# First-set raw weights in four own tiles, decode products at the pair's end, and several steps moved

## The chip, the cores and the metric

One core of a Trainium2 chip runs the kernel. The metric is the device time of one execution in microseconds (us); lower is better. Engines are named as in the profile: PE does matrix products, DVE and ACT element-wise work, POOL general work, SP issues most DMA transfers.

## The reference

One step of a decoder layer in float32. A prompt of 2048 tokens (width 1024) and 8 single new tokens ("samples", which carry states) go through one mixer: norm, one input projection to 8 groups of 512 columns, two recurrences, one output projection, a residual and a final norm.

```python
h = rmsnorm(x, norm_g)
rq, rk, rv, rg, hq, hf, hi, hgate = jnp.split(h @ w_in, 8, axis=-1)
rq = rotary(rq, pos);  rk = rotary(rk, pos) * RET_DK ** -0.5
o_ret, s_ret_new = chunked_decay_recurrence(rq, rk, rv, log_gamma, s_ret)   # one decay per head
o_ret = head_rmsnorm(o_ret, ret_g) * silu(rg)
logf = logaddexp(log(lb), log1p(-lb) + log_sigmoid(hf));  kin = (1 - lb) * sigmoid(-hf)
o_hg, s_hg_new = chunked_decay_recurrence(silu(hq), kin, hi, logf, s_hg)    # one decay per channel
o_hg = head_rmsnorm(o_hg, hg_g) * silu(hgate)
y = rmsnorm(x + concat([o_ret, o_hg]) @ w_out, final_norm_g)                # and the four new states
```

Each recurrence is S_t = diag(f_t) S_(t-1) + k_t v_t^T, o_t = S_t^T q_t, over 4 heads of 128 channels. For the samples it is one such step from the given states ("decode").

## The kernel before, in words

**Products.** float32 operands are split in two parts, high and low; a product is three matmuls (`three`, L350): high x high, high x low, low x high. Projections are done for a pair of token blocks at a time by a Strassen-Winograd scheme of seven products (`v_pair`, list `CHAIN`: A11 B11, A12 B21, S2 T2, S1 T1, S3 T3, S4 B22, A22 T4), each 12 matmuls of 128x512. B is weights, T sums of weights, A tokens, S sums of tokens.

**Stages.** 24 pairs run in three sets of eight: the first set (pairs 0 to 7) projects the value columns, the second and third the retention columns; beside the third set run the retention steps (`r_steps`, its p is the pair less 16). Then eight units (half, head) of the HGRN recurrence, whose projections, in groups of six matmuls, are the fill; then the output projection, again in pairs with seven products each.

**Order.** PE runs in the order of the code. In a set, `after[n]` lists what is called once product n of a pair has been written (half numbers: in the middle of the next). DVE, ACT and SP are put in order by a scheduler when the kernel is built; `behind(f)` has what f issues follow the last instructions of DVE, ACT and SP that are written so far. In the HGRN stage each unit's work is a list of (fraction, step), and `merge` writes a step into the fill once the fraction of the fill is done. `MOVE` shifts single steps there: key (half, head, level).

**Buffers.** A tile takes the next buffer of its pool and tag, and whoever writes it first waits for the last reader of the tile that had it. Pool `rawp` has six buffers of 512 KB for raw weights, raw tokens (xr) and sums (S). Pool `ps_o`, tag "o", has two buffers in the matrix engine's memory; the state updates (pu), the chunk outputs (po) and the decode products (pd4 to pd7, pgd) of the HGRN stage and of the first set take them in turn.

**First set.** Token blocks come in as xn; their squares (ACT, `stats_sum`) give the norms; PE spreads the row sums (prs). In pairs 2 to 5, `wg_load` loads two rows-of-blocks of the second set's raw weights (wgr, product B and its sums), `wg_decode` multiplies the samples by them (pgd, 16 small matmuls by `four`), and `wg_spool` makes their sums (`w_sums`, four DVE operations) and stores these (ws1T).

**HGRN.** The recurrence of a unit works in levels: bursts of 64 small products (plh) give scores of sub-blocks; after each, DVE updates kh and qqh in place and copies scores by a mask into Abh, and ACT copies kh and qqh (kepth) for the next. The burst of level 1 and of level 3 (`levels2`) of some units takes a decode product with it (`then_decode`, `d_mm`): dS times the sample's query, into pd; pd6 goes with unit (1,1), level 3. The outputs of the unit before run at the same time: puh (state), poh (output of a chunk; h100 is half 1, head 0, chunk 0), ACT squares of it, DVE obh (output times norm), PE poth (transposed).

**Retention and output.** `r_flip` transposes rk (pkt), `r_score` makes scores (par, DVE rA), `r_out` the outputs (por). `d_tr` transposes the decode outputs `do` (pdt); `wd_at` places it in an output pair.

## Time and profile before

| | us |
|---|---|
| median of three runs | 1028.8 (1026.54 to 1030.4) |
| the profiled execution | 1030.97 |
| its span (first to last instruction) | 1029.1 |
| PE busy | 1014.0 |
| DVE busy | 734.2 |
| ACT busy | 550.3 |
| POOL busy | 122.8 |

The profile comes from one execution; times in it are us from the span's start. Rows of the timeline are start, length, engine, line, operation, output<-inputs, shape and count; a bracket tells how long the engine stood idle before it and what it waited for. Waits are listed as engine, tile and line, released by engine, tile and line: total, number, longest. Buffer numbers are left out, so plh113 reads plh. The mean granted clock of PE is 0.998 of full.

### The profile page before, as it was taken

How to read it: one execution, taken by the hardware profiler on the slowest of the kernel's cores; microseconds unless marked ns; L12 is line 12 of the kernel's file. 1: busy time of each engine (PE TensorE's matmuls, PEld its weight loads, DVE VectorE, ACT ScalarE, POOL GpSimd, SP SyncE). 2: the span in 40 equal slices, each digit the busy share in tenths (PEclk: the TensorE clock that was granted, in tenths of full speed). 3: DMA queues.
4: the chain of work that ended last, by engine and by line, in shares of the span. 5: the costliest groups of instructions: out<-in, count | busy, mean ns of one | idle time of the engine just before them, and what ended most of it. 6: DMA issues, size and time to landing. Idle time of an engine off the chain costs nothing.

```text
span 1029.1 us, 21541 instructions
## 1 busy us (share of the span) xinstructions
PE 1014.0 (99%) x8366; PEld 841.7 (82%) x8366; DVE 734.2 (71%) x1353; ACT 550.3 (53%) x1211; POOL 122.8 (12%) x231
## 2 busy tenths in 40 slices
PE   9999999999999999999999999999999999999997
PEld 7767778887778888888888899898888878878775
DVE  7887666888675885576666768768768576667886
ACT  7863435735434765555564665667556476433242
POOL 0200001000000101111111100111022112301122
PEclk9999999999999999999999999999999999999999
DMA  8699998878999965567766697555864496565652
GB/s 290 210 327 330 332 334 275 326 263 313 312 326 304 359 238 184 189 226 247 233 222 205 210 334 268 193 185 200 283 216 133 129 362 227 180 252 204 227 186 103
DMA packets 151271, 255.63 MB, mean 248 GB/s; under 512 B 11424, under 2 KB 79280, under 8 KB 151040
## 3 DMA queue, kind: packets, MB, share of 16 engines
q1 hardware_dynamic: 141408, 225.03, 64.7%
q0 software_dynamic: 7440, 24.76, 6.3%
q10 hardware_dynamic: 2320, 4.46, 1.2%
q8 instruction: 66, 1.08, 0.4%
q14 instruction: 37, 0.30, 0.1%
HBM read 166.51 MB, written 87.69 MB: 247 GB/s over the span
## 4 chain that ended last, share of the span: by engine, by line
PE 82%; DMA 4%; DVE 1%; issue 0%; SPq 0%; POOLq 0%; ACT 0%; POOL 0%; DVEq 0%; ACTq 0%
PE po L350 10%; PE pjqh L1032 9%; PE pjfh L1032 8%; PE py L1659 4%; PE plh L1246 2%; PE pur L741 1%; PE par L734 1%; PE puh L1115 1%; PE por L747 1%; PE por L749 1%; PE poh L1131 1%; DMA oT1h<-t_dramh 1%; PE poh L1133 1%; PE pv20a L350 1%; PE pv21a L350 1%; PE pv22a L350 1%
## 5 line engine op out<-in xcount | busy, mean ns | idle before, releaser
L1032 PE MATMUL pjfh<-xh,w_h 128*128 128x512 f32 (+2 forms) x160 | 59.4, 372 | 0.0
L1032 PE MATMUL pjqh<-xh,w_h 128*128 128x512 f32 (+2 forms) x160 | 58.9, 368 | 0.0
L1226 ACT ACTIVATE kepth<-kh 128x1024 f32<-128x1024 f32 x24 | 25.4, 1060 | 62.0 <-DVE kh L1216 62.0
L1032 PE MATMUL pjqh<-xh,w_l 128*128 128x512 f32 (+2 forms) x160 | 55.7, 348 | 0.0
L1032 PE MATMUL pjfh<-xh,w_l 128*128 128x512 f32 (+2 forms) x160 | 55.7, 348 | 0.0
L1032 PE MATMUL pjfh<-xl,w_h 128*128 128x512 f32 (+2 forms) x160 | 55.6, 348 | 0.0
L1032 PE MATMUL pjqh<-xl,w_h 128*128 128x512 f32 (+2 forms) x160 | 55.6, 347 | 0.0
L1216 DVE TENSOR_TENSOR kh<-kh,fph 128x512 f32<-128x512 f32 x48 | 33.4, 696 | 22.8 <-PE plh L1246 19.8
L118 DVE TENSOR_TENSOR ab_l<-xr,ab_h 128x512 fp32r<-128x512 f32 (+1 forms) x40 | 37.5, 954 | 11.6 <-ACT ab_h L117 11.6
L772 DVE SCALAR_TENSOR_TENSOR obr<-por,omr,rg 128x128 f32<-128x128 f32 x64 | 18.0, 344 | 33.3 <-POOL omr L764 28.2
L762 ACT ACTIVATE obr<-por 128x128 f32<-128x128 f32 x64 | 16.8, 277 | 44.4 <-PE por L749 40.6
L117 ACT ACTIVATE ab_h<-xr 128x512 fp32r<-128x512 f32 (+1 forms) x40 | 32.4, 838 | 11.3 <-DVE xr L302 11.3
L1032 PEld LDWEIGHTS pjqh<-xh,w_h 128*128 128x128 f32 x160 | 30.4, 190 | 4.8 <-issue 1.2
L1032 PEld LDWEIGHTS pjfh<-xh,w_h 128*128 128x128 f32 x160 | 30.2, 189 | 4.1 <-issue 0.4
L1032 PEld LDWEIGHTS pjqh<-xh,w_l 128*128 128x128 f32 x160 | 30.1, 188 | 4.1
L1032 PEld LDWEIGHTS pjfh<-xh,w_l 128*128 128x128 f32 x160 | 30.1, 188 | 4.0
L409 ACT ACTIVATE vo<-vo 128x512 f32<-128x512 f32 x32 | 20.1, 629 | 24.7 <-DVE vo L403 10.8
L1219 DVE TENSOR_TENSOR qqh<-qqh,fph 128x512 f32<-128x512 f32 x48 | 32.8, 683 | 0.0
L1032 PEld LDWEIGHTS pjqh<-xl,w_h 128*128 128x128 f32 x160 | 30.2, 189 | 3.0
L1032 PEld LDWEIGHTS pjfh<-xl,w_h 128*128 128x128 f32 x160 | 30.2, 189 | 2.7
L302 DVE SCALAR_TENSOR_TENSOR xr<-xr,g_in,rb 128x256 f32<-128x256 f32 x64 | 27.1, 480 | 7.3 <-DMA xr<-in_x_t 4.2
L1659 PE MATMUL py<-woh,oc_h 128*128 128x512 f32 x64 | 26.6, 415 | 0.0
(1839 smaller groups left out, 3335.0 us busy)
## 6 DMA issues: line engine op xcount, KB each, us to landing
xr<-a_dram SPq DMA_DIRECT2D x24, 512.0 KB
S<-s_dram SPq DMA_DIRECT2D x24, 512.0 KB
xn<-in_x_prompt SPq DMA_DIRECT2D x32, 256.0 KB
xr<-in_x_t SPq DMA_DIRECT2D x16, 512.0 KB
a_dram<-xr SPq DMA_DIRECT2D x16, 512.0 KB
s_dram<-S SPq DMA_DIRECT2D x16, 512.0 KB
wgr<-in_w SPq DMA_DIRECT2D x16, 512.0 KB
xr<-a_dram SPq DMA_DIRECT2D x32, 256.0 KB
```

The lines of the kernel that those rows point to most:

```text
L117: act.activation(h, src, AF.Copy)
L118: dve.tensor_tensor(l, src, h.bitcast(F32), op=ALU.subtract)
L302: dve.scalar_tensor_tensor(r[:, k], r[:, k], g_in[:, kk : kk + 1], spread_to[i], op0=ALU.mult, op1=ALU.mult)
L350: pe.matmul(ps, xx, ww, start=(first and n == 0), stop=(last and n == 2), skip_group_check=more)
L409: act.activation(o, src, AF.Silu)
L772: dve.scalar_tensor_tensor(o[:, cc], po[:, h], ms[:, h : h + 1], rb_of[c, "g"][:, cc], op0=ALU.mult, op1=ALU.mult)
L1032: pe.matmul(ps, ww[:, kk], x[:, k, b0 : b0 + n], start=(k == 0 and i == 0), stop=(k == KT - 1 and i == 2),)
L1216: dve.tensor_tensor(kv[:, :, 0, :], kv[:, :, 0, :], two[:, :, 1:2].to_broadcast([P, nb, b]), op=ALU.mult)
L1219: dve.tensor_tensor(qv[:, :, 1, :], qv[:, :, 1, :], two[:, :, 0:1].to_broadcast([P, nb, b]), op=ALU.mult)
L1226: act.activation(ss[:, 512:], k[:, :HALF], AF.Copy)
L1246: pe.matmul(dst[32 * i : 32 * i + 32, c], kk, qq, start=True, stop=True)
L1659: pe.matmul(ps, o[:, kk], w[:, k % 4, i * 512 : (i + 1) * 512], start=(k == 0 and n == 0), stop=(k == KT - 1 and n == 2),)
```

## The change

It has six parts:

1. Six more small warm-up products (18 instead of 12).
2. In the first set, the raw weights of a pair (1 MB) lie in four tiles of their own (tags zh0, zl0, zh1, zl1, one buffer each) and come in four loads of 256 KB, instead of two loads of 512 KB into `rawp`. They are loaded after product 1, tied behind what is written so far, instead of after product 0. Decode products, sums and stores come after product 6, the pair's last, instead of after 4 (pair 3: 5).
3. The squares of the first half of a pair's tokens, and the load of the second half, move from after product 2 to after product 1 in pairs 3 to 5 (pair 2 had them there).
4. In the first retention step, `r_flip` and `r_score`/`r_update` move half a product later.
5. `MOVE` gets three entries: the bursts of unit (1,1) level 3, unit (1,2) level 1 and unit (0,3) level 1 come earlier in the fill.
6. `d_tr` moves from after product 4 of output pair 2 to after product 0 of output pair 3.

```diff
--- before.py
+++ after.py
@@ -82,7 +82,7 @@
     wu = ps_tr.tile([P, P], F32, tag="tr", name="wu")
     for n in range(14):
         pe.matmul(wu, ones, ones, start=True, stop=True)
-    for n in range(12):
+    for n in range(18):
         pe.matmul(wu[:32, :16], ones[:, :32], ones[:, :16], start=True, stop=True)
 
     zero = const.tile([P, 24], F32, name="zero")
@@ -500,11 +500,12 @@
             hi_lo(h, l, wr[k][:, ty])
 
     def w_sums(r0, r1):
-        dve.tensor_tensor(r0[:, 0], r0[:, 1], r0[:, 0], op=ALU.subtract)
-        dve.tensor_tensor(r0[:, 1], r1[:, 1], r0[:, 1], op=ALU.subtract)
-        dve.tensor_tensor(r1[:, 1], r1[:, 1], r0[:, 0], op=ALU.subtract)
-        dve.tensor_tensor(r1[:, 0], r1[:, 0], r1[:, 1], op=ALU.subtract)
-        return ("T2", r1[:, 1]), ("T3", r0[:, 1]), ("T1", r0[:, 0]), ("T4", r1[:, 0])
+        b11, b12, b21, b22 = (r[:, g] if hasattr(r, "shape") else r[g] for r in (r0, r1) for g in range(2))
+        dve.tensor_tensor(b11, b12, b11, op=ALU.subtract)
+        dve.tensor_tensor(b12, b22, b12, op=ALU.subtract)
+        dve.tensor_tensor(b22, b22, b11, op=ALU.subtract)
+        dve.tensor_tensor(b21, b21, b22, op=ALU.subtract)
+        return ("T2", b22), ("T3", b12), ("T1", b11), ("T4", b21)
 
     def wv_comb(k):
         for op, r in w_sums(wr[k], wr[k + 4]):
@@ -512,9 +513,14 @@
             hi_lo(h, l, r)
 
     def wg_load(n, k):
-        for kk in (k, k + 4):
-            wr[kk] = rawp.tile([P, 2, GW], F32, tag="raw", name=f"wgr{n}{kk}")
-            sp.dma_start(wr[kk].rearrange("p g n -> p (g n)"), a[f"w_{n}"][kk])
+        for j, kk in enumerate((k, k + 4)):
+            if n == 1:
+                wr[kk] = [vq.tile([P, GW], F32, tag=f"z{x}{j}", name=f"wgr{n}{kk}{x}") for x in "hl"]
+                for g, r in enumerate(wr[kk]):
+                    sp.dma_start(r, a[f"w_{n}"][kk, :, g * GW : (g + 1) * GW])
+            else:
+                wr[kk] = rawp.tile([P, 2, GW], F32, tag="raw", name=f"wgr{n}{kk}")
+                sp.dma_start(wr[kk].rearrange("p g n -> p (g n)"), a[f"w_{n}"][kk])
 
     pgd = {}
 
@@ -522,7 +528,8 @@
         if n not in pgd:
             pgd[n] = ps_o.tile([P, 256], F32, tag="o", name=f"pgd{n}")
         for kk in (k, k + 4):
-            four(pgd[n], xs[:, kk], wr[kk].rearrange("p a b -> p (a b)"), kk == 0, kk == KT - 1)
+            halves = wr[kk] if n == 1 else [wr[kk][:, g] for g in range(2)]
+            four(pgd[n], xs[:, kk], halves, kk == 0, kk == KT - 1)
 
     def wg_spool(n, k):
         for op, r in w_sums(wr[k], wr[k + 4]):
@@ -587,7 +594,10 @@
     def four(ps, x, w, first, last):
 
         for j in range(4):
-            pe.matmul(ps[32 * j : 32 * j + x.shape[1]], x, w[:, j * 256 : j * 256 + 256], start=first, stop=last)
+            ww = w[j // 2] if isinstance(w, list) else w[:, j // 2 * 512 : j // 2 * 512 + 512]
+            pe.matmul(
+                ps[32 * j : 32 * j + x.shape[1]], x, ww[:, j % 2 * 256 : j % 2 * 256 + 256], start=first, stop=last
+            )
 
     pvd = []
 
@@ -817,9 +827,9 @@
             put(0.5 if p > 1 else 1.5, lambda: r_turn(ca - 2))
         if p < N_V:
             put(3, lambda: r_load(ca, "q"), lambda: r_load(ca, "v"))
-            d = 0 if p else 0.5
+            d = 0 if p else 1
             put(3.5 + d, lambda: r_flip(ca))
-            put(4 + d if p else 6, lambda: r_load(ca, "g"))
+            put(4 if p else 6, lambda: r_load(ca, "g"))
             put(5 if 0 < p < N_V - 1 else 4.5 + d, lambda: r_score(ca), lambda: r_update(ca))
             if p:
                 put(6, lambda: r_out(ca), lambda: r_load(ca + 1, "q"), lambda: r_load(ca + 1, "v"))
@@ -937,7 +947,7 @@
                 at = 6
             after[at] += [lambda i=i: tok_load(i + 2)]
         if i + 2 < N_V:
-            after[1 if i == 2 else 2] += [lambda i=i: behind(lambda: stats_sum(i + 2, 0)), lambda i=i: stats_load(i + 2, 1)]
+            after[1] += [lambda i=i: behind(lambda: stats_sum(i + 2, 0)), lambda i=i: stats_load(i + 2, 1)]
             after[4] += [lambda i=i: behind(lambda: stats_sum(i + 2, 1)), lambda i=i: stats_end(i + 2)]
             if i + 3 < N_V:
                 after[5] += [lambda i=i: stats_load(i + 3, 0)]
@@ -948,8 +958,11 @@
             after[2] += [decode_spread]
         if m < 3:
             if 2 <= j < 6:
-                after[0] += [lambda m=m, k=j - 2: wg_load(m, k)]
-                after[5 if i == 3 else 4] += [lambda m=m, k=j - 2: wg_decode(m, k), lambda m=m, k=j - 2: wg_spool(m, k)]
+                if m == 1:
+                    after[1] += [lambda m=m, k=j - 2: behind(lambda: wg_load(m, k))]
+                else:
+                    after[0] += [lambda m=m, k=j - 2: wg_load(m, k)]
+                after[6 if m == 1 else 4] += [lambda m=m, k=j - 2: wg_decode(m, k), lambda m=m, k=j - 2: wg_spool(m, k)]
             if j == 7:
                 after[0] += [lambda m=m: behind(lambda: wg_decode_out(m))]
                 for n, (_, op, _) in enumerate(CHAIN):
@@ -1174,7 +1187,7 @@
         dve.tensor_copy(old, pools["S"][hd - NH])
         return old
 
-    MOVE = {(0, 0, 1): 0.065, (0, 1, 3): 0.065, (0, 2, 1): 0.065, (1, 0, 1): 0.125, (1, 3, 1): 0.11}
+    MOVE = {(0, 0, 1): 0.065, (0, 1, 3): 0.065, (0, 2, 1): 0.065, (1, 0, 1): 0.125, (1, 3, 1): 0.11, (1, 1, 3): -0.1, (1, 2, 1): -0.065, (0, 3, 1): -0.06}
 
     def hgrn_rec(half, h, u):
         name = f"h{half}{h}"
@@ -1874,7 +1887,8 @@
         wd_at[i] += [(st_, lambda n=n: wd_load(2 * n)), (st_, lambda n=n: wd_load(2 * n + 1))]
         i, st_ = ((4, 3), (5, 0), (5, 4), (6, 1))[n]
         wd_at[i] += [(st_, lambda n=n: wd_mm(2 * n)), (st_, lambda n=n: wd_mm(2 * n + 1))]
-    wd_at[2] += [(0, d_ms), (2, d_rs), (4, d_tr)]
+    wd_at[2] += [(0, d_ms), (2, d_rs)]
+    wd_at[3] += [(0, d_tr)]
     wd_at[p0] += [(1, lambda: t3_split(0)), (2, lambda: t3_split(1))]
     wd_at[5] += [(0, lambda: dec.update(y=y_load(a["x_sample"], NB, "d")))]
     wd_at[6] += [(2, wd_out)]
```

What moves on the engines is shown at two places. On PE, around the burst of unit (1,1), level 3 (`plh` is the burst, `pd` is pd6, `poh` the output of chunk 101, `pjqh` and `pjfh` the fill). Before:

```order
L1032 MATMUL pjqh_0_8713<-xl_7115,w_h 128x512
L1032 MATMUL pjqh_0_8713<-xh_7114,w_l 128x512
L1246 MATMUL plh_8732<-kepth_8627 32x16 x32
L1246 MATMUL plh_8732<-qqh_8027,kh_8026 32x16 x32
L590 MATMUL pd_8808<-dS_8497,dqp 32x256 x4
L1032 MATMUL pjqh_0_8713<-xh_7114,w_h 128x512
```

After:

```order
L1144 MATMUL poh_8706<-v_8088,Ah 128x128
L1146 MATMUL poh_8706<-sth_8533,qqh_7538 128x128
L1259 MATMUL plh_8727<-kepth_8649 32x16 x32
L1259 MATMUL plh_8727<-qqh_8049,kh_8048 32x16 x32
L598 MATMUL pd_8803<-dS_8519,dqp 32x256 x4
L1045 MATMUL pjqh_0_8819<-xh_7136,w_h 128x512
```

The burst and pd6 stood between two groups of fill; now they follow directly on poh101, and pd6 still follows directly on the burst.

On DVE at the same place (`obh` of poh_8657 or poh_8679 is chunk 100's, of poh_8684 chunk 101's; the masked copies read plh113). Before:

```order
L1146 SCALAR_TENSOR_TENSOR obh_8720<-poh_8657,orsh_8675,v_8064 128x128 x4
L845 TENSOR_TENSOR dv_8710<-dv_8710,dk 128x1024
L1216 TENSOR_TENSOR kh_8026<-kh_8026,fph_8429 128x32x16
L1219 TENSOR_TENSOR qqh_8027<-qqh_8027,fph_8429 128x32x16
L1252 COPY_PREDICATED Abh_8454<-lmask,plh_8732 128x16x8
L1252 COPY_PREDICATED Abh_8454<-lmask,plh_8732 128x8x16
L1216 TENSOR_TENSOR kh_8026<-kh_8026,fph_8429 128x16x32
L1219 TENSOR_TENSOR qqh_8027<-qqh_8027,fph_8429 128x16x32
L1146 SCALAR_TENSOR_TENSOR obh_8816<-poh_8684,orsh_8702,v_8068 128x128 x4
```

After:

```order
L1187 COPY oldh_8983<-S_5677 128x128
L1229 TENSOR_TENSOR kh_8048<-kh_8048,fph_8451 128x32x16
L1232 TENSOR_TENSOR qqh_8049<-qqh_8049,fph_8451 128x32x16
L1265 COPY_PREDICATED Abh_8476<-lmask,plh_8727 128x16x8
L1265 COPY_PREDICATED Abh_8476<-lmask,plh_8727 128x8x16
L1229 TENSOR_TENSOR kh_8048<-kh_8048,fph_8451 128x16x32
L1232 TENSOR_TENSOR qqh_8049<-qqh_8049,fph_8451 128x16x32
L1159 SCALAR_TENSOR_TENSOR obh_8826<-poh_8679,orsh_8697,v_8086 128x128 x4
L855 TENSOR_TENSOR dv_8816<-dv_8816,dk 128x1024
```

Chunk 100's four obh stood ahead of the two updates and the masked copies; now they stand behind the two updates, the copies and two more updates.

On SP, from the stores of one pair's sums to the next pair's raw weights, in pair 5 (`ws1T` stores of sums, `wgr` raw weights, `xr` and `xn` tokens, `v_dram` results). Before:

```order
L529 DMA ws1T_128<-wgr_1171 128x512
L529 DMA ws1T_129<-wgr_1169 128x512
L529 DMA ws1T_127<-wgr_1169 128x512
L529 DMA ws1T_130<-wgr_1171 128x512
L344 DMA v_dram_94<-vo_1309 128x512
L242 DMA xr_1312<-in_x_t 128x1024
L242 DMA xr_1313<-in_x_t 128x1024
L263 DMA xn_1316<-in_x_prompt 128x512
L263 DMA xn_1317<-in_x_prompt 128x512
L344 DMA v_dram_93<-vo_1332 128x512
L517 DMA wgr_1350<-in_w 128x1024
L517 DMA wgr_1352<-in_w 128x1024
```

After:

```order
L536 DMA ws1T_128<-wgr16l 128x512
L536 DMA ws1T_129<-wgr12l 128x512
L536 DMA ws1T_127<-wgr12h 128x512
L536 DMA ws1T_130<-wgr16h 128x512
L344 DMA v_dram_93<-vo_1381 128x512
L263 DMA xn_1392<-in_x_prompt 128x512
L263 DMA xn_1393<-in_x_prompt 128x512
L520 DMA wgr13h<-in_w 128x512
L520 DMA wgr13l<-in_w 128x512
L520 DMA wgr17h<-in_w 128x512
L520 DMA wgr17l<-in_w 128x512
L312 DMA a_dram_107<-xr_1314 128x1024
```

The two loads of 512 KB behind the xr and xn loads became four of 256 KB, behind the second two xn loads (which stood later); the xr loads and the first two xn loads stand ahead of the stores.

## The prediction

> **What bounds the kernel now.** I read the page's busy rows first, then the list of what PE (the matrix engine) waited for, then single stretches of the timeline. The busy rows say that PE is the bound nearly everywhere.
>
> ```profile
> span 1029.1 us, 21541 instructions
> PE 1014.0 (99%) x8366; PEld 841.7 (82%) x8366; DVE 734.2 (71%) x1353; ACT 550.3 (53%) x1211; POOL 122.8 (12%) x231
> ```
> ```profile
> PEclk9999999999999999999999999999999999999999
> ```
>
> PE works 1014 of 1029 us at full granted clock, and the change neither removes nor adds products that count. So the time can move only by waits of PE that go and waits that come. Those that the change touches are these (total us, times, longest us):
>
> ```profile
> PE pgd L590 <- DMA wgr<-in_w: 2.7, 5, 0.7
> PE pkt L726 <- DVE rk L375: 1.4, 1, 1.4
> PE pdt L1396 <- DVE do L1392: 1.2, 1, 1.2
> ...
> PE prs L288 <- POOL rs_all L114: 0.6, 1, 0.6
> ```
>
> Together 5.9 us: all that can be won here is little over 0.5% (5.1 us), about what a measurement of this kernel can tell from no change.
>
> **Decode products of the first set (pgd).** Before, they stand in the middle of pairs 2, 4 and 5 and late in pair 3, and wait for their weights. Of pair 2 and of pair 3, PE's timeline (start, length):
>
> ```profile
> 71.59 0.62 PE L590 MATMUL pgd<-wgr,pk 128*8 128x256 f32 x8 [0.40 <-DMA wgr<-in_w]
> 72.80 0.62 PE L590 MATMUL pgd<-wgr,pk 128*8 128x256 f32 x8 [0.60 <-DMA wgr<-in_w]
> 73.35 0.50 PE L350 MATMUL pv2c<-B22h,s21h 128*128 128x512 f32 x1
> ```
> ```profile
> 95.60 1.05 PE L590 MATMUL pgd<-wgr,pk 128*8 128x256 f32 x16
> 96.58 0.50 PE L350 MATMUL pv3a<-T4h,ab_h 128*128 128x512 f32 x1
> ```
>
> Pair 3 waits for nothing: from its burst to the next product are 0.98 us. Pair 2's burst takes 1.76, 0.78 more, after an idle 0.40: it loses 1.18 where its idle rows add up to 1.0. By that ratio the 2.7 us of the list are 3.2 us of PE time. All of it goes if the weights are there at the pair's end.
>
> Whether they are, SP decides, which issues in order. A tile is used by the products, then by four sums, then by a store, and only then loaded again. The old order had such a chain too, and the chain view of pair 5 shows it:
>
> ```profile
> 123.00 5.90 DMA ws1T<-wgr
> 128.90 0.02 issue
> 128.92 8.37 DMA wgr<-in_w
> ```
>
> The new order of SP puts two token loads (xn) ahead of the four weight loads of pairs 4 and 5. Their buffers are freed by ACT's squares, which in the new order follow ACT's eviction p of the pair's fourth product. In pair 5 of before these are the rows (ACT's p, SP's two xn, and the square that one of them released):
>
> ```profile
> 134.02 0.58 ACT L390 ACTIVATE p<-pv5c 128x512 f32<-128x512 f32 x1
> ```
> ```profile
> 140.43 1.08 SPq L263 DMA_DIRECT2D xn<-in_x_prompt  x2
> ```
> ```profile
> 144.88 0.63 ACT L269 ACTIVATE xn<-xn 128x512 f32<-128x512 f32 x1 [0.60 <-DMA xn<-in_x_prompt]
> ```
>
> On this clock: p ends at 134.6, two squares of some 0.8 end at 136.2, the xn loads are issued by then, and four weight loads at 0.54 (1.08 for two) bring the last to 138.5. The decode products come three products of 12 matmuls after the fourth; at 0.23 us a matmul (the fence around plh below) that is 134.0 + 8.3 = 142.3. So the last load has 3.8 us. The nearest row for 256 KB in this stretch is xn itself: issued at 140.43, it released ACT at 144.88, 4.4 us. That makes a wait of some 0.6 us in each of pairs 4 and 5. The far row is the 8.37 us of wgr, behind a fuller queue: 4.6 us each. I take the nearer one, since in the new order only the two xn stand in the queue ahead: 1.2 us of new wait, ends 0 and 9.2. Pairs 2 and 3 have no eviction ahead of their loads; nothing is counted.
>
> The Trainium skill, "DMA: Bandwidth & Descriptors", section "Anatomy of one DMA", fits 2.0 us plus bytes over 436 GB/s to one transfer of GpSimd's queue; an estimate by it for 256 KB is 2.6 us, which fits into 3.8 and would take 1.2 us off the sum. The xn row's 4.4 us, in the traffic of this stretch, decides against it here.
>
> **Squares earlier.** The first half's row sums come a product earlier for the tokens of pairs 5 to 7, so prs should not wait: -0.6, ends 0 and -0.6.
>
> **First retention step half a product later.** rk came 1.4 us after PE asked for pkt; six matmuls fill just that. Scores and updates (par) move as far, so they run at the same clock time as now, but por does not move and comes 1.4 us earlier:
>
> ```profile
> 370.48 0.86 DVE L736 SCALAR_TENSOR_TENSOR rA<-par,pk 128x128 f32<-128x128 f32 x3
> ```
> ```profile
> 374.09 1.05 PE L747 MATMUL por<-rv,rA 128*128 128x128 f32 x8
> ```
>
> por would come at 372.7, rA is done at 371.3, or 1.2 to 2.4 later if one or two splits of DVE slip in ahead (1.2 each, by the oT3l row below). I take -1.0, ends -1.4 and -0.7.
>
> **d_tr three products later.** pdt then stands well behind `do`: -1.2. Next in line are the splits oT3l, which end at 918.99 now:
>
> ```profile
> 916.63 2.36 DVE L118 TENSOR_TENSOR oT3l<-oT3l,oT3h 128x1024 fp32r<-128x1024 f32 x2 [0.71 <-ACT oT3h L117]
> ```
> ```profile
> 919.33 0.39 PE L350 MATMUL po<-oT3l,op2S2h 128*128 128x512 f32 x1
> ```
>
> Their product would ask at 918.1, when the first half (to 917.8) is done; -1.2 stands, the other end is -0.3.
>
> **Three level bursts joined to neighbours.** Groups of small fp32 products cost an entry and an exit, as around plh here, where the pace is 0.23:
>
> ```profile
> 789.50 0.39 PE L1032 MATMUL pjqh<-xl,w_h 128*128 128x512 f32 x1
> 789.73 0.39 PE L1032 MATMUL pjqh<-xh,w_l 128*128 128x512 f32 x1
> 790.05 0.70 PE L1246 MATMUL plh<-kepth 128*32 128x16 f32 x62
> ```
> ```profile
> 791.70 0.50 PE L1032 MATMUL pjqh<-xh,w_h 128*128 128x512 f32 x1
> 792.04 0.40 PE L1032 MATMUL pjqh<-xl,w_h 128*128 128x512 f32 x1
> ```
>
> 0.32 and 0.34 instead of 0.23 make 0.2 us a join; three are 0 to -0.6, and I take -0.4.
>
> **The new wait: pd6.** The burst of unit (1,1), level 3, takes the decode product pd6 with it, tied behind it. pd6 needs one of two buffers; its turn gives it poh100's, which is free when DVE has made the four obh of that chunk. Before, DVE had them done at 788.4, and pd6 ran at 791.1 with no wait:
>
> ```profile
> 787.29 1.12 DVE L1146 SCALAR_TENSOR_TENSOR obh<-poh,orsh,v 128x128 f32<-128x128 f32 x4 [2.44 <-POOL orsh L114]
> 788.33 1.22 DVE L845 TENSOR_TENSOR dv<-dv,dk 128x1024 f32<-128x1024 f32 x1
> 791.37 0.69 DVE L1216 TENSOR_TENSOR kh<-kh,fph 128x512 f32<-128x512 f32 x1 [1.82 <-PE plh L1246]
> 791.98 0.69 DVE L1219 TENSOR_TENSOR qqh<-qqh,fph 128x512 f32<-128x512 f32 x1
> 792.58 0.62 DVE L1252 COPY_PREDICATED Abh<-lmask,plh 128x128 f32<-128x128 uint8 x2
> 793.19 0.69 DVE L1216 TENSOR_TENSOR kh<-kh,fph 128x512 f32<-128x512 f32 x1
> 793.80 0.69 DVE L1219 TENSOR_TENSOR qqh<-qqh,fph 128x512 f32<-128x512 f32 x1
> 794.41 1.12 DVE L1146 SCALAR_TENSOR_TENSOR obh<-poh,orsh,v 128x128 f32<-128x128 f32 x4
> ```
> ```profile
> 791.15 0.62 PE L590 MATMUL pd<-dS,dqp 128*32 128x256 f32 x6
> ```
>
> In the new order of DVE chunk 100's obh stand behind six instructions of which the first waits for plh113, and PE goes straight from plh113 to pd6. The rows from 791.37 on are that very chain, with chunk 101's obh at its end: to 794.41 + 1.12 = 795.53 it takes 4.16 us. PE stands still for that, the projection fill queued behind pd6. ACT's part in it, a copy of kh between the two updates, follows four short squares of poh101, which are done in time. I take +4.2; the ends are 3.4 (the chain to 794.41 and one obh) and 5, if ACT comes late.
>
> **The rest.** Six more warm-up products:
>
> ```profile
> 6.05 0.93 PE L86 MATMUL wu<-ones 128*32 128x16 f32 x24
> ```
> ```profile
> 7.66 0.50 PE L350 MATMUL pv<-wv_l,ab_h 128*128 128x512 f32 x1 [0.23 <-DVE wv_l L118]
> ```
>
> The twelve of now (two rows each) take 0.9 us; six more take 0.45 ahead of the first real product, and PE waits for wv_l at the second, 7.66, in any case: 0, ends 0 and +0.4. dS7 and dv7 are loaded later, past a store on SP; pd7, a unit later, needs them long after; 0, ends 0 and +2, the latter if DVE stands at dv7 with chunk 101's obh behind it.
>
> **Sum.** -3.2 + 1.2 - 0.6 - 1.0 - 1.2 - 0.4 + 4.2 = -1.0 us. The profiled execution took 1030.97 us (its span and 1.9 us around it), 2.2 above the median of the runs; so 1030.0 against it, and 1027.8 as a median.
>
> **The rivals.**
>
> *No stall at pd6* (its buffer free in time): 5.2 less than nothing changed, 1023.6, and 1022.4 if the weights are in time too. For it: before, pd6 had 2.7 us to spare. Against: the new order shows six instructions ahead, which need plh113 itself.
>
> *Slower: the weights come late at the pair's end.* The place is SP in pairs 4 and 5: xn and its squares, then the loads. With 8.4 us from issue to landing PE waits 4.6 us in each, 9.2 instead of 1.2: 1035.8. From 4.9 us on (1.1 each) nothing is left of the gain, from 7.5 us on the kernel is slower by 0.5%. For it: 8.37 is a row of this very load. Against: SP's order had 3 MB of stores and loads between the first ws1T store and that load; the new one waits for those stores to land and has 0.5 MB of xn ahead.
>
> *The change does nothing at pgd*: the stretch is bound by DMA and 3.2 us of waits merely move. Then 1029.8. For it is the row
>
> ```profile
> 129.00:154.00 25.00, 24.36 (x120) 18.98 (x119) 15.28 (x26) 9.63 (x18) 1.08 (x3) 1.00 0.94 336
> ```
>
> with its DMA share of 0.94; against it, that the loads are now due 5 us later in the pair.
>
> *PE restarts slowly.* A gap of 4.2 us is three times the longest wait listed. If matmuls ran at half pace for as long after it, 2 to 4 us come on top: 1030 to 1032. The clock row shows no such case, since no gap was as long. The Trainium skill, "TensorE: Matmul & The Clock Gate", Part 1, says that PE's clock halves after one idle window of about 3.4 us; by that rule a gap of 4.2 may or may not cover a whole window. No run here shows it yet.
>
> **Chances.** The forecast 0.60, with a range of its own of 1025.5 to 1030; no stall 0.13; weights late 0.12; nothing at pgd 0.08; slow restart 0.07. Of no stall, most lies under 1023.7, so faster 0.11; of late weights, most lies over 1033.9, so slower 0.10; the rest, 0.79, within 0.5%. The range 1023 to 1033.5 leaves out the far parts of two rivals.
>
> **What would show it.** In the profile after: a wait of pd for obh of about 4.2 us, the longest of PE; pkt, pdt and prs gone from the list; pgd under 1.5 us; por with at most 0.6 of new wait. I am wrong if pd is not in the list, if pgd's waits are over 3 us, or if the granted clock falls behind pd6.

## The result, and the profile after

| | before | after |
|---|---|---|
| median, us | 1028.76 (1026.54 to 1030.4, 6 runs) | 1037.67 (1035.74 to 1040.7, 6 runs) |
| profiled execution, us | 1030.97 | 1037.73 |
| PE busy, us | 1014.0 | 1018.9 |

The changed kernel takes 1.0087 of the time before (95%: 1.0066 to 1.0107): 8.9 us slower, where 1.0 us faster was forecast, and above the range.

The page after (span, busy time, granted clock in 40 slices):

```profile
span 1036.0 us, 21588 instructions
...
PE 1018.9 (98%) x8378; PEld 844.7 (82%) x8378; DVE 734.4 (71%) x1353; ACT 551.2 (53%) x1211; POOL 124.3 (12%) x231
...
PEclk9999999999999999999999999999999999999998
```

The 12 new rows of small products explain 0.4 us of busy time, yet PE is busy 4.9 us longer. So part of the loss is in PE working slowly, and the clock row in forty slices is too coarse to say where. The list of PE's waits after (total us, times, longest):

```profile
PE pd L598 <- DVE obh L1159: 4.3, 1, 4.3
PE wu L84 <- POOL ones L78: 1.1, 1, 1.1
PE potr L790 <- DVE obr L782: 1.1, 1, 1.1
PE pv2c L350 <- ACT p L390: 0.8, 1, 0.8
PE pgd L598 <- DMA wgr16h<-in_w: 0.8, 1, 0.8
PE pgd L598 <- DMA wgr<-in_w: 0.6, 1, 0.6
```

pkt, pdt and prs are gone, as forecast; pd is there with the forecast size. potr (the transposed output of a retention step) and pv2c (one of the result tiles of pair 2's products; p and s are ACT's copies that free such tiles) are new and were not forecast. pgd of the first set keeps 1.0 us (wgr16h, and 0.2 of wgr12l further down the list); the 0.6 is the second set's. The timeline of PE around pd6:

```profile
789.83 0.67 PE L1259 MATMUL plh<-qqh,kh 128*32 128x16 f32 x58
794.75 0.67 PE L598 MATMUL pd<-dS,dqp 128*32 128x256 f32 x8 [4.25 <-DVE obh L1159]
795.36 0.80 PE L1045 MATMUL pjqh<-xh,w_h 128*128 128x512 f32 x1
795.95 0.63 PE L1045 MATMUL pjqh<-xl,w_h 128*128 128x512 f32 x1
796.38 0.63 PE L1045 MATMUL pjqh<-xh,w_l 128*128 128x512 f32 x1
...
798.81 0.40 PE L1045 MATMUL pjqh<-xh,w_l 128*128 128x512 f32 x1
799.04 0.40 PE L1045 MATMUL pjqh<-xh,w_h 128*128 128x512 f32 x1
```

and of DVE, with the chain that pd6 waits for:

```profile
790.55 0.69 DVE L1229 TENSOR_TENSOR kh<-kh,fph 128x512 f32<-128x512 f32 x1 [3.73 <-PE plh L1259]
...
793.58 1.12 DVE L1159 SCALAR_TENSOR_TENSOR obh<-poh,orsh,v 128x128 f32<-128x128 f32 x4
795.54 1.23 DVE L855 TENSOR_TENSOR dv<-dv,dk 128x1024 f32<-128x1024 f32 x1 [0.84 <-DMA dv<-vd_dram]
```

The wait is the one forecast. What was not in the sum stands behind it: products of 128x512 start 0.43 us apart (795.95, 796.38) instead of 0.23 (798.81, 799.04). Stretches with busy times (PE, PEld, DVE, ACT, POOL), then PEclk and the DMA share:

```profile
790.00:795.00 5.00, 0.74 (x63) 0.56 (x55) 4.11 (x10) 4.04 (x12) 1.56 (x2) 1.00 0.75 235
795.00:797.00 2.00, 2.00 (x12) 1.36 (x5) 1.46 (x3) 1.49 (x3) 0.67 (x2) 0.56 0.91 362
797.00:799.00 2.00, 2.00 (x7) 1.57 (x6) 1.97 (x6) 0.90 (x2) 0.43 (x1) 0.59 0.19 64
799.00:801.00 2.00, 2.00 (x10) 1.61 (x9) 1.19 (x1) 0.00 (x0) 0.00 (x0) 1.00 0.00 0
```

The granted clock falls to 0.56 and 0.59 behind the gap and is back at 1.00 from 799 on; PE counts as busy all the while. Over these products it costs 1.5 us (start to start less 0.23). This was the prediction's own sign of being wrong.

The decode products of pair 4 after (the two xn loads and the last of the four weight loads on SP, then PE):

```profile
113.11 1.92 SPq L263 DMA_DIRECT2D xn<-in_x_prompt  x2
...
116.51 0.42 SPq L520 DMA_DIRECT2D wgr16l<-in_w  x1
...
119.86 0.60 PE L598 MATMUL pgd<-wgr12h,pk 128*8 128x256 f32 x4
120.71 0.61 PE L598 MATMUL pgd<-wgr12l,pk 128*8 128x256 f32 x4 [0.24 <-DMA wgr12l<-in_w]
122.10 0.60 PE L598 MATMUL pgd<-wgr16h,pk 128*8 128x256 f32 x4 [0.78 <-DMA wgr16h<-in_w]
122.73 0.61 PE L598 MATMUL pgd<-wgr16l,pk 128*8 128x256 f32 x4
123.27 0.50 PE L350 MATMUL pv5a<-wv_h,ab_h 128*128 128x512 f32 x1
```

The last load is issued at 116.51, 3.35 us before PE asks for the first tile, and its tile is used at 122.73. The burst takes 3.4 us from start to start (119.86 to 123.27), where pair 3 before took 0.98.

Start times of PE's same products in the two profiles account for the 6.9 us between the spans: +0.9 up to the first set, +0.4 in pairs 2 to 7, +0.4 in pair 8, +0.8 at pgd of the second set (pair 11), -1.6 at pkt, +1.1 at potr, +5.5 from the level bursts to behind pd6, -1.2 at pdt, +0.5 behind the last product.

### The profile page after: what moved, and what is told of

It reads as the page before. It is cut to its first block, busy times and chain, and to the rows that moved or that the text cites. A ratio compares the mean times of both kernels' runs of the same rounds, so it can differ in the third digit from the quotient of the medians.

```text
span 1036.0 us, 21588 instructions
## 1 busy us (share of the span) xinstructions
PE 1018.9 (98%) x8378; PEld 844.7 (82%) x8378; DVE 734.4 (71%) x1353; ACT 551.2 (53%) x1211; POOL 124.3 (12%) x231
## 5 line engine op out<-in xcount | busy, mean ns | idle before, releaser
L1150 ACT ACTIVATE jkh<-poh 128x128 f32<-128x128 f32 x64 | 17.7, 276 | 20.2 <-PE poh L1146 18.8
```

The costliest lines, as they stand in the source:

```text
L1150: act.activation(jk, po[:, j], AF.Square, accum_out=ms[:, j : j + 1])
```

## The experiments

The theories. **Stall**: the entry (1,1,3) of `MOVE` costs its wait, 4.2 us, and a slow restart on top. **Cheap parts**: squares, retention step, d_tr and the two other entries gain 1 to 2 us. **Weights**: loading them late and using them at the pair's end gains little or loses. **One execution**: the waits pkt and pdt were peculiar to the profiled execution, which was 2.2 us above the median. **Warm-up**: free, or not. Each ratio is to the kernel before, run beside it, and has a 95% interval. Differences in us are those of medians; the kernel before had medians from 1027.9 to 1028.9 in the different rounds, so a difference between two experiments is good to one or two us.

**e1, the changed kernel without that entry.**

```diff
-    MOVE = {..., (1, 1, 3): -0.1, (1, 2, 1): -0.065, (0, 3, 1): -0.06}
+    MOVE = {..., (1, 2, 1): -0.065, (0, 3, 1): -0.06}
```

> The changed kernel without its MOVE entry for (1,1,3). Theory 1, the stall at pd6 and a halved clock behind it: the entry costs 4.4 us of wait and about 1.5 us of matmuls at half pace (intervals 0.43 instead of 0.23 us in the changed kernel's trace), less 0.2 us of a joined burst; so 5.7 us come back, about 1032 us, and no PE wait over 1.5 us is left. Rival, the stall alone costs: 4.2 us back, about 1033.5. Rival, the wait was hidden or only moved: under 1 us back.

Measured 1031.41, ratio 1.0031 (1.0016 to 1.0045). The entry costs 6.3 us here, and 3 us are left that are not the entry's.

**e2, the kernel before with that entry alone.**

```diff
-    MOVE = {..., (1, 3, 1): 0.11}
+    MOVE = {..., (1, 3, 1): 0.11, (1, 1, 3): -0.1}
```

> The kernel before with only the MOVE entry for (1,1,3). Theory 1 (wait and halved clock): 5.7 us slower, about 1034.5 us, a PE wait of pd for obh of 4.3 us, granted clock under 0.7 in the 3.4 us behind it. Rival, wait alone: 4.2 us slower, about 1033, clock 1.00 all through. Rival, the wait needs the other edits: no change, 1028.8.

Measured 1034.4, ratio 1.0059 (1.0043 to 1.0075): +6.1. In its profile pd waits 4.25 us for obh, and PE then runs at half pace for six products.

**e3, the changed kernel with the weights part undone** (loads into `rawp` after product 0, decode products after 4).

```diff
-            if n == 1:
+            if n == 9:      # true for no n, so the loads go to rawp; the same in wg_decode
-                    after[1] += [lambda m=m, k=j - 2: behind(lambda: wg_load(m, k))]
+                after[0] += [lambda m=m, k=j - 2: wg_load(m, k)]
-                after[6 if m == 1 else 4] += ...
+                after[5 if i == 3 else 4] += ...
```

> The changed kernel with the first set's raw weights, loads and decode products as in the kernel before (all other parts kept). Theory 2, the weights come late at the pair's end and the decode products no longer cover the eviction p: the new placement costs about 1.2 us against the old, so about 1036.5 us, with the old waits of pgd for wgr (2.7 us) back and the wait of pv2c for p gone. Rival, the placement gains as predicted (2 us) and the loss lies elsewhere: about 1039.7 us.

Measured 1038.61, ratio 1.0098 (1.0082 to 1.0115): no faster than the changed kernel, where 1.2 us faster was expected. Undoing the weights in this company gains nothing; alone they are measured in e12.

**e4, the kernel before with the retention step and d_tr moved**, and **e5, the kernel before once more**.

```diff
-            d = 0 if p else 0.5
+            d = 0 if p else 1
-    wd_at[2] += [(0, d_ms), (2, d_rs), (4, d_tr)]
+    wd_at[2] += [(0, d_ms), (2, d_rs)]
+    wd_at[3] += [(0, d_tr)]
```

> The kernel before with only two moves: the first retention step half a product later and d_tr in the next output pair. Theory 3, both waits simply go: 1.5 and 1.2 us, 2.7 us faster, about 1026.0 us, no wait of pkt and pdt in the list. Rival, a later step takes it back (por, potr or the oT3l product): 0 to 1 us faster, 1028 to 1028.8 us.

> The kernel before once more, for a second profile. Theory 4, the waits of pkt (1.4 us) and pdt (1.2 us) that the prediction took off stand in the one profiled execution, which was 2.2 us above the median, and not in a typical one: at least one of the two is missing here (the run with only the (1,1,3) entry, which touches neither, showed neither). Rival: both stand in the list again with over 1 us each.

e4: 1027.24, ratio 0.9997 (0.9986 to 1.0007): 1.0 us by the medians, 0.3 by the ratio, whose interval takes in no gain at all, where 2.2 was forecast. e5's profiled execution took 1027.83, and this is its list of PE's waits:

```profile
PE pgd L590 <- DMA wgr<-in_w: 1.8, 3, 0.9
PE wu L84 <- POOL ones L78: 1.1, 1, 1.1
PE par L734 <- DVE xl L118: 0.9, 1, 0.9
PE prs L288 <- POOL rs_all L114: 0.6, 1, 0.6
```

No pkt, no pdt: of 5.9 us that the prediction hoped to win from, 2.6 were not in this execution of the same kernel. Of the eight profiles of kernels that keep these two steps (before, e2, e5, e9, e12 to e15), only that of before has pkt, and only two have pdt (e12 1.5 us).

**e6, the changed kernel once more.**

> The changed kernel once more, for a second profile. Theory 1: the wait of pd for obh is again 4.2 to 4.4 us and some 3 us of halved pace follow within it (three of three profiles with the stall so far). Rival, the slow pace is chance: clock 1.00 behind the stall. Waits of pgd for wgr: by theory 2 (late by the order of SP) over 1.5 us in pairs 4 and 5 together again; rival (chance of one execution): none, as in the changed kernel without the (1,1,3) entry.

1037.86; pd waits 4.25 us again and ten products behind it run at half pace (2.1 us); potr does not wait in this one.

**e7, the kernel before with the cheap parts alone**: e4's edit, the squares after product 1, and the entries (1,2,1) and (0,3,1).

```diff
-            after[1 if i == 2 else 2] += [lambda i=i: behind(lambda: stats_sum(i + 2, 0)), ...]
+            after[1] += [lambda i=i: behind(lambda: stats_sum(i + 2, 0)), ...]
-    MOVE = {..., (1, 3, 1): 0.11}
+    MOVE = {..., (1, 3, 1): 0.11, (1, 2, 1): -0.065, (0, 3, 1): -0.06}
```

> The kernel before with the squares a product earlier, the retention step, d_tr, and the entries for (1,2,1) and (0,3,1), so all of the change but the warm-up products, the weights and the (1,1,3) entry. If these parts are worth their waits: 1.0 us as in the run with two of them, 0.6 for prs, 0.3 for two joins, about 1026.3 us. Rival, one of them costs what the changed kernel without the (1,1,3) entry lost in all (3 us slower than before although two parts gain): over 1030 us, and the wait of potr for obr (1.3 us) in the list.

1026.74, ratio 0.9987 (0.9974 to 0.9999): 1.6 us faster than before, the best version, and 11 us faster than the changed kernel. Its margin is smaller than what one median can tell.

**e8, the changed kernel with pd6 in another buffer.**

```diff
-            pt = ps_o.tile([P, 256], F32, tag="o", name=f"pd{hd}")
+            pt = (ps_tr if hd == 6 else ps_o).tile([P, 256], F32, tag="tr" if hd == 6 else "o", name=f"pd{hd}")
```

> The changed kernel with pd6 in a buffer of the other pool (tag tr), nothing else. Theory 1, the wait is for poh100's buffer: pd6 waits no more, poth100 some products later waits at most 1 us for the same obh, the clock stays full; 5 us faster than the changed kernel, about 1032.5. Rival, the order of PE at this place is itself bad (the next product waits as long for DVE): under 2 us faster, a wait of 3 us or more at poth.

1033.71, ratio 1.0048 (1.0034 to 1.0063): 4.0 us come back, not 6. The wait of pd is gone; the next one is seen in PE's and DVE's timelines:

```profile
794.79 1.22 DVE L855 TENSOR_TENSOR dv<-dv,dk 128x1024 f32<-128x1024 f32 x1 [1.50 <-DMA dv<-vd_dram]
795.93 1.12 DVE L1159 SCALAR_TENSOR_TENSOR obh<-poh,orsh,v 128x128 f32<-128x128 f32 x4
```
```profile
796.12 0.55 PE L1166 MATMUL poth<-ident,obh 128*128 128x128 f32 x3 [2.15 <-DVE dv L855]
```

DVE stands 1.50 us at dv7, which SP loads later, with chunk 101's obh behind it. PE waits 2.15 us and goes on at 796.12, as dv7 ends (796.01). Why three of four transposes waited for dv7 and not for an obh the trace does not show. This is of the size of the prediction's far end of dv7 (+2). In the changed kernel DVE waits there too (0.84 us, row 795.54 above), but after PE is released, and PE does not wait for it.

**e9, the kernel before with 18 small warm-up products.**

```diff
-    for n in range(12):
+    for n in range(18):
```

> The kernel before with 18 small warm-up products instead of 12, nothing else. Open is where some 4 us of the changed kernel's loss lie: with old weights it was 1038.6, although the cheap parts (1026.7) and the (1,1,3) entry (6.1 us slower) add up to 1032.9; only the warm-up is left. Theory 5, the warm-up costs that: about 1033 us. Rival, it costs at most its own length, 0 to 0.4 us: 1028.3 to 1028.7, and parts do not add up.

1030.88, ratio 1.0026 (1.0017 to 1.0035): 2.7 us for a part costed at nothing. PE's first real product starts at 8.40, against 6.93 and 7.68 in the two profiles of before; but with 24 small products (e13 below) it starts at 8.72, and that kernel is no slower. The wait that neither profile of before has is 570 us later, 1.2 us at potr. The timelines of before and of e9 there (POOL's store of unit 0's outputs; in e9 also ACT, which writes that tile again):

```profile
569.57 0.81 POOL L783 DMA_DIRECT2D o_dram<-obr  x1 [6.79 <-DVE u L439]
```
```profile
567.86 0.81 POOL L783 DMA_DIRECT2D o_dram<-obr  x1 [7.08 <-DVE u L439]
572.21 0.28 ACT L762 ACTIVATE obr<-por 128x128 f32<-128x128 f32 x1 [1.19 <-DMA o_dram<-obr]
575.18 1.10 PE L780 MATMUL potr<-ident,obr 128*128 128x128 f32 x4 [1.16 <-DVE obr L772]
```

and the DMA view of 568 to 574 us of before and of 567 to 573 us of e9 (last number: us from issue to landing):

```profile
o_dram<-obr POOLq DMA_DIRECT2D x1, 256.0 KB, 2.6
```
```profile
q8 instruction: 1, 0.02, 1.5%
...
o_dram<-obr POOLq DMA_DIRECT2D x1, 256.0 KB, 4.2
```

The store takes 1.6 us longer, and ACT, DVE and PE wait for it in turn. In both kernels one packet of the instruction queue q8 passes here: in e9 at 569.31, as the store's data begins, taking 1.5 us; before at 572.67, 0.9 us after the store's data has ended. Six small products more make PE's program longer at its head, so the places where its instructions are fetched fall elsewhere in the work. The rest is behind PE's last product, which starts at 1021.71 in before and at 1019.78 in e9: before ends 7.4 us after that (span 1029.1), e9 9.0 us (span 1028.8). 1.2 at potr and 1.6 at the end are 2.8. Most of the 1.6 arises at 966 us. ACT's rows there in e13 and in e9 (ACT waits for the loads of `or`, outputs read back, which SP issues from 957.97 on in e13 and from 958.18 on in e9):

```profile
964.74 0.63 ACT L117 ACTIVATE op6A22ks<-or 128x512 fp32r<-128x512 f32 x1 [3.58 <-DMA or<-o_dram]
```
```profile
966.14 0.63 ACT L117 ACTIVATE op6A22ks<-or 128x512 fp32r<-128x512 f32 x1 [4.76 <-DMA or<-o_dram]
```

In e9 a packet of q8 that takes 2.6 us starts at 961.26, while these loads run; in e13 it has passed by 960. ACT, and with it the chain of ACT, POOL and DVE that ends the kernel, is 1.2 us later in e9 from there on; PE is not.

**e13, e14, e15: the kernel before with other warm-ups.** 24 small products; 6; and 8 large with 18 small, as many instructions as before.

```diff
-    for n in range(14):
+    for n in range(8):      # e15; 14 in e13 and e14
-    for n in range(12):
+    for n in range(18):     # e15; 24 in e13, 6 in e14
```

> The kernel before with 24 instead of 12 small warm-up products, nothing else; 18 of them cost 2.6 us. Theory (position): 18 products make the head of PE's program 12 instructions longer, and a 16 KB fetch of instructions then falls into the store of unit 0's obr (4.17 to 4.58 us to land instead of 2.6), and another into the output stage. With 24 the fetches come 12 instructions earlier still, some 2.8 us, so the one near unit 0 ends before the store begins: store back to 2.6 us, no potr wait, median 1028.0 to 1029.3. Rival (price by itself): each six products cost 2.6 us at the start or by the clock's phase: 1033 to 1033.5. Third (chance positions): no rule, the tail after the last product anywhere from 7.4 to 9.7 us.

> The kernel before with 6 instead of 12 small warm-up products. Theory (position): the fetches come 12 instructions later than before, further behind the store, which still lands in 2.6 us: median 1028 to 1029, no potr wait, tail 7.4. Rival (price by itself): 2.6 less, 1025.7.

> The kernel before with 8 large and 18 small warm-up products instead of 14 and 12: as many instructions as before. Theory (position): the fetches come where they came before: store 2.6 us, no potr wait, tail 7.4, median 1028.3, plus at most 0.5 if the clock doubles later. Rival (the 18 small products themselves): 1030.9 as with 18 of 32.

1028.59, ratio 0.9997 (0.9983 to 1.0011); 1029.51, 1.0001 (0.9981 to 1.0021); 1029.41, 1.0006 (0.9991 to 1.0022). None costs anything that can be told, none has a wait at potr, and the ends are 7.4 us in all three. Twice as many new products as in e9 cost nothing, and e9's own 18 cost nothing when six large ones go: it is where the fetches fall, not the products. In e13 the packet comes at 569.70 and the store's data starts at 570.54; it lands 3.0 us after issue, in time. A rival is that the scheduler, which orders the other engines when the kernel is built, made another order with 18 products. The traces exclude it: DVE, ACT, SP and POOL run in the same order in e9 and e13, row by row. (e15 is less clean: its scheduler changed the order of some instructions of the first set.)

**e10 and e11, the cheap parts with the entry (1,1,3), and with the weights part; e12, the kernel before with the weights part.** The edits are those of e2 and, the other way round, of e3.

> The kernel with the cheap parts (1026.7 us) and the (1,1,3) entry: the changed kernel but for warm-up and weights. If the entry costs the same everywhere: 6.1 us more, about 1032.9 us. Rival, together with the moved neighbours (the potr wait of 1.3 us, a longer stretch at half pace) it costs more: 1036 us or over, and then the warm-up is not to blame.

> The kernel with the cheap parts and the first set's weights in four tiles with decode products at the pair's end: the changed kernel but for warm-up and the (1,1,3) entry. Theory 2 (late by SP's order, cover of p gone): 1 to 1.5 us over the cheap parts alone, about 1028. If the weights carry all of the 4.6 us that the changed kernel without the entry has over the cheap parts: about 1031.4. If the warm-up carries it: 1026.7.

> The kernel before with only the weights part (four tiles, loads after product 1, decode products at the pair's end; squares as before). As predicted, 2 us faster (1026.3), when squares and xn are not ahead of the loads. Theory 2: the loads are still late behind the stores, and p has lost its cover: 1 us slower or more, 1029.3 to 1031, waits of pv2c for p (0.8) in the list.

e10: 1032.11, ratio 1.0041 (1.0029 to 1.0053), 5.4 over e7: the entry's price (5.4 here, 6.1 in e2, 6.3 in e1) is the same in any company, as far as these runs tell. e11: 1033.27, 1.0047 (1.0031 to 1.0064), 6.5 over e7 by the medians, 6.0 by the ratios. e12: 1028.92, 1.0015 (1.0003 to 1.0026), 1.0 over before by the medians, 1.5 by the ratio. So the weights cost 1 to 1.5 us alone and some 6 beside the cheap parts; in e11 a wait of pv8a and half pace in pair 8 are new. PE's waits of e12:

```profile
PE prs L288 <- POOL rs_all L114: 3.3, 3, 1.2
...
PE pv2c L350 <- ACT p L390: 1.1, 1, 1.1
```

pgd is not in this list: its waits went, as the prediction said. But prs waits 3.3 us where it waited 0.6 before, and pv2c 1.1.

**e16, the changed kernel with 12 warm-up products; e18, the same with the squares where they were; e17, the changed kernel with 24.**

```diff
-    for n in range(18):
+    for n in range(12):     # e16 and e18; 24 in e17
-            after[1] += [lambda i=i: behind(lambda: stats_sum(i + 2, 0)), ...]
+            after[1 if i == 2 else 2] += [lambda i=i: behind(lambda: stats_sum(i + 2, 0)), ...]   # e18
```

> The changed kernel with 12 small warm-up products as before. If the warm-up's price adds to the rest: 1037.7 - 2.6 = 1035.1, no potr wait, tail 7.4. If the parts overlap (after, the stalls at pd6 and in the first set give the store time): 1036.5 to 1037.7. By the parts alone (1028.3 - 1.5 for the cheap ones, +5.4 for the entry, +1.0 to +6.5 for the weights): 1033 to 1038.7; under 1034 the weights cost little in this company, over 1037 their price with the squares holds.

> The changed kernel with 12 warm-up products and the squares after product 2 as before. With the squares earlier SP has four of the second set's wg1B loads behind the dg_dram store of pair 7, with the squares late three. Theory (order of SP): the fourth load behind the store is what made pv8a wait 2.1 us and run at half pace (4.65 us in all); without it pair 8 has none of that, and the time falls from 1039.8 to 1035 to 1036, with prs waits of some 3 us in the first set (as when the weights part stood alone) within this. Rival (the fetch of instructions inside the issue of wg1B is the whole cause): the stall stays, 1039 or more.

> The changed kernel with 24 small warm-up products. Theory (position): the fetch of PE's instructions near unit 0's store ends before it, as with 24 in the kernel before (store 3.05 us, no potr wait), and near pair 8 it comes before the wg1B loads, as with 18: no stall there. Then 1037.7 less up to 2.6: 1035 to 1036.5. Rival (the 2.6 us belong to the kernel before alone): 1037 to 1038.5. Against both: a stall of pv8a behind wg1B as with 12 products: 1039 to 1040.

e16: 1039.78 (1037.07 to 1043.1), ratio 1.0095 (1.0065 to 1.0125): no gain; potr's wait is gone and pair 8 waits instead. e18: 1034.69, 1.0061 (1.0046 to 1.0075): less than e16 in every one of five runs each, 5.1 us by the medians, 3.5 by the ratios. e17: 1036.79, 1.0074 (1.006 to 1.0088): 0.9 under the changed kernel, which these runs do not tell apart; no potr, no stall in pair 8. Of PE's waits of e16, and SP's timeline of pair 7 in e16 and in e18:

```profile
PE pv8a L350 <- ACT s L390: 2.1, 1, 2.1
```
```profile
170.43 0.30 SPq L546 DMA_DIRECT2D dg_dram<-gd  x1
170.83 0.35 SPq L344 DMA_DIRECT2D v_dram<-vo  x1
171.24 4.48 SPq L576 DMA_DIRECT2D wg1B<-in_w  x4
```
```profile
166.91 0.37 SPq L576 DMA_DIRECT2D wg1B<-in_w  x1
171.20 0.31 SPq L546 DMA_DIRECT2D dg_dram<-gd  x1
171.60 0.34 SPq L344 DMA_DIRECT2D v_dram<-vo  x1
172.00 3.72 SPq L576 DMA_DIRECT2D wg1B<-in_w  x3
```

With weights and squares both moved, the scheduler puts four of the second set's weight loads (wg1B) behind the store dg_dram, which waits until 170.4; with the squares late it puts three there, and one goes out 4 us earlier. ACT splits the weights and is late with s, which PE waits for. With 18 or 24 products the same order of four costs only 0.4 and 0.2 us, so a second condition is needed; in e16 a fetch of PE's instructions (171.21, 1.3 us) falls into the issue of the first of the four loads, which takes 1.7 us instead of 0.4. The twenty profiles bear out that both are needed. Four loads behind the store and a fetch in their issue: pv8a waits 2.1 us (e11, e16). Four loads, and the fetch over before the first: at most 0.3 (after, e1, e6, e8, e17). Three loads, with a fetch in their issue (eleven profiles, e18 among them) or without one (e13, e14): no wait of pv8a.

## Why the prediction was wrong

The sum gave -1.0, and +8.9 was measured. Four of its terms failed. The weights were to gain 2.0 net and cost 1.0; pkt and pdt were to gain 2.2 and gained at most 1.0; the entry (1,1,3) was to cost its wait of 4.2 and cost 6.1 with the half pace behind it; squares and warm-up were to gain 0.6 and add 3.0. These four measured prices add up to 9.1; each is good to one or two us, so that they meet 8.9 so closely is luck. Behind the third lies a premise of the first paragraph, that the time can move only by waits of PE: PE's busy time rose by 4.9 us.

**The stall, right in place, cause and size.** 4.16 us were worked out, 4.25 measured, eight times in eight profiles with that entry and pd6 in its old buffer; e8 shows that the buffer is the cause. The chain of DVE, now with chunk 100's obh at its end, took the time of the rows of before.

**The slow restart, taken as a rival at 0.07, always came.** In all eight profiles the products behind the 4.25 us run at half pace, and lose 1.1 to 2.3 us. With it the entry cost 5.4 to 6.3 us (e10, e2, e1) instead of 4.2. The failed step is that the rival was weighed by the lack of a case in the trace of before; the gap forecast was itself the case. The Trainium skill, "TensorE: Matmul & The Clock Gate", Part 1, halves the clock after one idle window of about 3.4 us; the runs agree on the length, and do not bear out that all of the window must be idle (below). e8's single gap of 2.15 us was followed by full pace. But in e16, 2.07 us of idle time, 1.4 us behind another of 0.39, led to this:

```profile
192.00:194.00 2.00, 2.00 (x6) 1.58 (x5) 2.00 (x3) 2.00 (x3) 0.00 (x0) 0.50 1.02 409
```

So a bound on a single gap is not what these runs show. The clock records kept with the traces show more. Up to PE's last product the clock changes only at points that lie 3.41 us, or a multiple of it, apart. With PE's idle time summed between two such points, the clock stayed full after every stretch with up to 1.86 us idle (the most is e8's, over whose gap such a point falls), and fell after all ten with 1.98 or more: e11 1.98 and e16 2.07 in pair 8; at pd6 e17 2.10, e10 2.52, e3 2.81, after 2.94, e6 2.98, e2 3.16, e16 3.27; only in e18 all 3.41. (One more fall, in e15 at its start, came after 1.12 us idle among the small warm-up products.) The half pace lasts one such stretch (after, e2, e10, e18), or two where the second has much idle time too (0.99 us or more at pd6 in e3, e6, e16, e17), which is why it cost 1.1 us in one profile and 2.3 in another.

**pkt and pdt, -1.0 and -1.2: mis-sized.** Both waits stood in a profile that took 2.2 us more than the median, and e5's has neither. e4 gives at most 1.0 for both.

**pgd, -3.2 and +1.2: the waits went, the gain did not.** Alone the part costs 1.0 us instead of gaining 2.0 (e12), though pgd waits no more there. The step that failed is that all of 3.2 us would be won: the burst in mid-pair had given other engines time, and without it prs waits 2.7 us more (e12) and pv2c, for ACT's eviction p, 0.8 to 1.4 us in seven of the nine profiles with the part (0.3 in e11, none in e1). The sum has neither. That the burst was the cover is the likely reading; it was not tried apart. The second term was too small too: the 4.4 us from issue to landing, taken from one xn, were 5 to 6 from issue to use for the loads that PE waited for in pairs 4 and 5 (wgr16l, issued at 116.51, is used at 122.73). And the argument, which looked at pairs 4 and 5 alone, left out what the change does to SP's order two pairs later.

**prs, -0.6: gone as said**, but the squares that remove it cost 3.5 to 5.1 us beside the weights with 12 warm-up products (e16 against e18). The step "earlier is free" looked at ACT and POOL and not at SP's queue in pair 7. This interaction of two parts is in no term.

**Warm-up, 0 to +0.4: 2.7 alone (e9).** The step looked at the first real product. That does start later (8.36 in the changed kernel, 6.93 before), but so it does with 24, at no price that e13 can tell (its interval is 1.4 us to either side). What cost was the position of instruction fetches. In the changed kernel it is not a term of its own: with 12 products the loss comes back in pair 8 (e16).

**The joins, -0.4, and dv7, 0 to +2.** The joins' ends hold: two bursts that stall nothing move PE by -0.05 to -0.3 us in the two profiles. dv7's far end is real and shows once pd6 no longer stalls (e8).

**The sum as measured.** The kernel before with all parts but the earlier squares and the six warm-up products takes 1034.7 (e18), 6.1 over before: that is the entry's price alone, so weights and cheap parts cancel. Squares and warm-up together add 3.0 to 1037.7, of which neither can be given a share: with the warm-up alone undone the loss comes back in pair 8 (e16), and the squares alone undone was not run. The rival that ended slower, late weights, had its direction right and its place wrong: PE lost not 4.6 us in each of pairs 4 and 5 but 2.4 and 0.9, and in some versions more in pair 8.

## What to carry to other kernels

Price a forecast stall with what follows it: here each idle gap of 4.25 us cost 1.1 to 2.3 us more of products at half pace, counted as busy, and two short gaps close together did the same. Before a wait is taken off, ask which other engine needed that time: here two waits took the place of the one that went. Before a wait is counted as winnable, see it in a second execution, above all when the profiled one is slower than the median. When one part of a change moves loads, read the order of the loading queue some pairs on with all the other parts in place, since two harmless moves made a late load together.

## What the runs showed that was not expected

Fetches of PE's instructions are DMA traffic. The page of the changed kernel has them as a queue of their own (packets, MB, share):

```profile
q8 instruction: 66, 1.08, 0.4%
```

That is 16 KB each. That they are PE's is read from their place: near unit 0's store the packet starts 3.1 us after the store's issue in before, e5 and e15, whose PE programs are equally long, 1.5 in e9 (12 instructions more), 0.6 in e13 (24 more) and 8.2 in e14 (12 fewer). In the changed kernel a packet takes 1.0 us in the median and 2.0 at the worst; e9 has one of 2.6. In the five of twenty profiles in which one starts while the data of unit 0's store (256 KB) is under way (after, e1, e3, e8, e9), the store lands 4.2 to 4.6 us after issue and potr waits 1.1 to 1.5. In the other fifteen potr does not wait, and the store lands after 2.6 to 3.0 where the trace tells. Other traffic can do the same: the next such store of before lands after 4.2 with no fetch near it. Adding or removing a few instructions at the head of the program moves all later fetches against the work: 6, 12 and 24 small products give 1028 to 1030 us, 18 give 1030.9. The Trainium skill, "Runtime: NRT & Kernel Launch", section "Instruction fetch mechanics", has fetches in blocks of 16 KiB, whose cost is mostly hidden; the size agrees, and in e9 the cost was not hidden.
